# A two-layer hybrid decoder step on one core: the sample group's new convolution columns are copied by ScalarE out of PSUM, query norms get a higher scheduling priority, six weight subtractions move to GpSimd

## The chip, the cores and the metric

The kernel runs on one core of a Trainium2 chip. The metric is the device time of one execution in microseconds (us); the time of a kernel is the median of its runs. Engines are named as the profile names them: PE (TensorE matmul), PEld (its weight loads), DVE (VectorE), ACT (ScalarE), POOL (GpSimd) and SP (SyncE, here a queue that starts DMAs). A q behind a name (ACTq, SPq) is the engine's sequencer, which starts DMAs.

## The reference

Two layers of a decoder trunk run on 544 tokens: a prompt of 512 and a sample group of 8 sequences with 4 new tokens each (32). Each layer is, in short:

```python
mod = silu(c) @ w_ada + b_ada                         # shift, scale and gate, per sequence
h = rmsnorm(x, norm1) * (1 + sc1) + sh1
q, k, v, qi, ki, wi, pool_u, z, xbc, dt_raw, gates = split(h @ w_in)
q = rope(rmsnorm(q, q_norm), pos)                     # the query norms
o_attn = sparse_attention(q, k_all, v_all, qi, ki_all, wi, pos, topk)
o_pool = pool_mix(pool_u, ...)
xbc, conv_state = causal_dwconv(xbc, conv_prev, conv_w, conv_b)    # width 4
o_ssd = ssd_mix(z, silu(xbc), dt_raw, h0, ...)
x = x + g1 * ((sum of gated branches) @ w_out)
h2 = rmsnorm(x, norm2) * (1 + sc2) + sh2
u, fconv_state = causal_dwconv(h2 @ ffn_up, fconv_prev, ffn_conv_w, ffn_conv_b)   # width 3
a, gg = split(u)
x = x + g2 * ((silu(gg) * a) @ ffn_down)
```

A causal convolution of the sample group reads the 3 (or 2) columns of each sequence's saved state and the 4 new columns behind them.

## The kernel before, in words

Activations lie with channels on the 128 partitions and the 544 tokens along the row, in two halves of 272 columns. PE does all products with weights in fp32 by three fp32r products: `weights` (L348 to L358) loads a 128x1024 tile by an SP DMA into a buffer `raw` (4 buffers, also used for tiles of w_ada and for key-value pages), ACT copies the high part `wh` (L177, the line of a helper for copies), DVE subtracts and gives the low part `wl` (L357); `wh` and `wl` have 3 buffers each. `gemm` (L360 to L373) multiplies one weight tile: 8 blocks x 3 products x 2 halves are 48 matmuls of 272 columns into one PSUM tile `psg`, of which there are 2 (L126, L185). `gemm2` (L375 to L392) does two weight tiles side by side at the start of a stage; its matmuls have line L388. It is called by `project` (in layer 0 with tiles prepared earlier) and by `ffn` for its first pair.

`conv` (L886 to L905) takes a finished `psg`. ACT copies it to `cu` (L177) and writes the scaled start of the sum `cacc` (L894). POOL copies the 32 new sample columns of `cu` into the tile `sti` behind the saved state (L896), and the last columns into `sto` (L897), which goes out. DVE adds the shifted products: L901 for the prompt, L904 for the sample columns, from `sti`. It runs 136 times: 24 tiles of xbc and 44 of the feed-forward, per layer. Then ACT takes the tanh `th` (L910) of those that need SiLU, and DVE multiplies (L911). In the feed-forward, tiles come in pairs, `a` and `gg`; every fourth pair a new `sti` is taken, and 8 small DMAs on ACT's queue load the saved state into it (L1628).

`ada` (L238 to L283) computes the modulation of a later stage from w_ada in pieces between other work: a generator loads tiles of w_ada (L255), multiplies them with the conditioning (L262, on PE), and is moved on one step by `pump` at the start of each `gemm`. A norm at a stage's end ends in an inverse square root by three Newton rounds on DVE (L304 to L312; L309 to L311 are one round); its result goes to PE (L468). In `attention`, the query norms use the same rounds; the sample group's factors are then copied by DVE to `qbc` (L1369) and transposed by PE (L1374). At that time DVE also runs the top-k search for the sample group: MAX8 (L861) and MATCH_REPLACE8 (L862) in turn.

The order of instructions on each engine is set by a scheduler when the kernel is built: it goes by modelled times, and by priorities where more than one instruction is ready. `high_priority(offset=WPRI)` lifts what stands under it. Each engine then works in its order; an instruction that waits holds what is behind it.

Of the kernel before, what the change touches and what calls it, by code (L numbers as in the profile page):

```python
# [103 lines left out]
class Prog:  # L104
# [134 lines left out]
    def ada(self, l, s, first=False):  # L239
# [8 lines left out]
        for c in range(4):  # L248
            ps = self.P("ada1")
            for pair in range(2):  # L250
                raws = []
                for z in (2 * pair, 2 * pair + 1):
                    with self.tc.high_priority(offset=WPRI):
                        raw = self.wr.tile([128, 1024], F32, name="raw", tag="raw")
                        nc.sync.dma_start(raw, a["w_ada"][l, s, 4 * c + z])  # L255
                    raws.append(raw)
                    if z % 2 == 0:
                        yield

                prods = []  # L260
                for k4 in range(4):
                    prods.append(nc.tensor.matmul(ps[32 * k4:32 * k4 + 32, :], self.sc[:, 4 * pair + k4, :],  # L262
                                     raws[k4 // 2][:, (k4 % 2) * 512:(k4 % 2) * 512 + 512],
                                     start=(pair == 0), stop=(pair == 1)))
                if pair == 0:
                    if turn:
                        turn(prods[-1].ins)
                        turn = None
                    yield
            if turn:  # L270
                turn(prods[-1].ins)
            row = self.t("adarow")
            self.copy("ada2", row[:, :512], ps)
            turn = self.ada_turn(row, dst[:, c], bias[:, c], first)
            if first or c == 3:
                turn(None)
                turn = None
            yield
# [68 lines left out]

    def weights(self, src, n):  # L348
        nc = self.nc
        z = self.nw = (self.nw + 1) % 4  # L350
        with self.tc.high_priority(offset=WPRI):
# [4 lines left out]
            self.copy("weights2", wh[:, :n], raw[:, :n])  # L356
            self.last_wl = self.E("weights1").tensor_tensor(wl[:, :n], raw[:, :n], wh[:, :n].bitcast(F32), op=OP.subtract).ins  # L357
        return wh, wl  # L358
# [15 lines left out]

    def gemm2(self, srcs, rhs, done=None):  # L375

# [3 lines left out]
        K = len(rhs)  # L380
        ws, self.pre = self.pre or [self.weights(src, K * 128) for src in srcs], None
        os_ = [self.G() for _ in srcs]
# [206 lines left out]
    def project(self):  # L589
        nc, a, l = self.nc, self.a, self.l  # L590
        par, mod, _ = self.par[l]
        h = self.h
        o, ok = self.gemm2([self.w(l, W_KI), self.w(l, W_K)], h)
        kd, self.ki = self.t("kd"), self.t("ki")
# [293 lines left out]
    def conv(self, o, par, wb, nt, bb, st, so, i, width):  # L888
# [5 lines left out]
        nc.scalar.activation(self.v2(acc), self.g2(o), AF.Identity, scale=wb[:, W - 1:W], bias=bb)  # L894
        new = u[:, 512:].rearrange("p (b t) -> p b t", b=8)
        self.E("conv1").tensor_copy(st[:, i, :, W - 1:], new)  # L896
        self.E("conv2").tensor_copy(so[:, i, :], u[:, 513 - W:])  # L897
# [403 lines left out]
    def attention(self):  # L1301
# [29 lines left out]
        def qnorm(sqs, c0):  # L1331
            mk = yield from self.ssq(sqs, "mq")
            self.newton(mk, self.s([128, 5, 8], "rsq_u8"), rq[:, :, c0:c0 + 8])
            yield
# [33 lines left out]
        for p in range(2):  # L1368
            self.E("attention7").tensor_copy(bc[p][:32, :512].rearrange("p (i e d) -> p i e d", i=4, e=2),  # L1369
                                  rq[:32, 4, 8 * p:8 * p + 8].rearrange("p (i e) -> p i e", e=2)[:, :, :, None]  # L1370
# [239 lines left out]
    def ffn(self):  # L1610
# [7 lines left out]
        for ci, n in enumerate(CH):  # L1618
            fs = []
            for jj in range(n):  # L1620
# [8 lines left out]
                if j == 0:  # L1629
                    o, o2 = self.gemm2([self.w(l, W_UP), self.w(l, W_UP + 1)], h)  # L1630
                else:
                    o = self.gemm(self.w(l, W_UP + 2 * j), h)
# [200 lines left out]
```

## Time and profile before

| what | value |
|---|---|
| median of 3 runs | 3163.01 us (3154.23 to 3165.09) |
| profiled execution, its own time | 3159.91 us |
| its span | 3158.1 us |
| PE busy | 3037.2 us (96%), 24136 matmuls |
| DVE, ACT, POOL busy | 71%, 40%, 28% |
| mean granted TensorE clock | 0.98 |

The span is the profile's own, from the first instruction to the last; 1.8 us lie around it. The profiled execution is 3.1 us below the median of the runs. Busy shares are means over all stages.

### The profile page before, as it was taken

The page shows a single profiled execution, that of the slowest core. Times are in us where ns is not written, and L with a number is a line of the kernel's source. Part 1 is how long each engine was busy: PE and PEld are TensorE (multiplying, and loading weights), DVE is VectorE, ACT ScalarE, POOL GpSimd, SP SyncE. Part 2 cuts the span into 40 slices and gives each one's busy share as a digit, 9 for nine tenths or more (in the row PEclk, how much of TensorE's full clock was granted, in tenths as well). Part 3 has the DMA queues.
Part 4 walks back from the last instruction along what each step waited for, and adds up shares of the span by engine and source line. Part 5 has one row for each costly group of instructions (what it writes and reads, how often), then busy time and mean ns, then how long its engine had stood idle before and what let it go on. Part 6 is the DMA issues. An engine that isn't in the chain of part 4 may idle for free. (4 is left out here: it accounts for less than half of the span.)

```text
span 3158.1 us, 62620 instructions
## 1 busy us (share of the span) xinstructions
PE 3037.2 (96%) x24136; PEld 2791.9 (88%) x24136; DVE 2235.4 (71%) x4879; ACT 1261.9 (40%) x2240; POOL 881.0 (28%) x1273
## 2 busy tenths in 40 slices
PE   7999999999999999999989999999999899999999
PEld 4987998999986789998989878989999857899999
DVE  5687878679988656454566878786799885564554
ACT  4344443333336534343443344343333364342432
POOL 1363445521121003111223635455211110121211
PEclk9999999999999999999999999999999899999999
DMA  6332332345543443545333323223333244333322
GB/s 234 107 110 75 113 95 99 113 137 185 190 125 122 162 143 102 162 153 170 94 117 107 107 78 116 93 90 123 99 132 116 79 136 152 98 90 90 86 97 76
DMA packets 303100, 376.81 MB, mean 119 GB/s; under 512 B 177362, under 2 KB 186930, under 8 KB 302802
## 3 DMA queue, kind: packets, MB, share of 16 engines
q1 hardware_dynamic: 116514, 315.94, 29.7%
q10 hardware_dynamic: 181216, 42.05, 6.6%
q0 software_dynamic: 5072, 14.83, 1.3%
q8 instruction: 190, 3.11, 0.4%
q14 instruction: 108, 0.88, 0.1%
HBM read 330.34 MB, written 33.79 MB: 115 GB/s over the span
## 5 line engine op out<-in xcount | busy, mean ns | idle before, releaser
L371 PE MATMUL psg<-hh,wh 128*128 128x272 f32 x4064 | 859.0, 291 | 9.1 <-ACT cacc L894 4.9
L177 ACT ACTIVATE wh<-raw 128x1024 fp32r<-128x1024 f32 (+2 forms) x434 | 425.0, 980 | 1107.1 <-PE psg L371 752.1
L371 PE MATMUL psg<-hl,wh 128*128 128x272 f32 x4064 | 850.0, 289 | 0.0
L371 PE MATMUL psg<-hh,wl 128*128 128x272 f32 x4064 | 847.6, 290 | 0.0
L357 DVE TENSOR_TENSOR wl<-raw,wh 128x1024 fp32r<-128x1024 f32 (+2 forms) x434 | 509.5, 1174 | 334.2 <-ACT wh L177 329.6
L371 PEld LDWEIGHTS psg<-hh,wh 128*128 128x128 f32 x4064 | 642.8, 190 | 35.4 <-issue 14.0
L371 PEld LDWEIGHTS psg<-hh,wl 128*128 128x128 f32 x4064 | 640.4, 189 | 9.8 <-issue 7.2
L371 PEld LDWEIGHTS psg<-hl,wh 128*128 128x128 f32 x4064 | 640.4, 190 | 6.8 <-issue 4.7
L896 POOL COPY sti<-cu 128x32 f32<-128x32 f32 x136 | 85.4, 628 | 522.7 <-ACT cu L177 522.5
L901 DVE SCALAR_TENSOR_TENSOR cacc<-cu,half,cacc 128x511 f32<-128x511 f32 x144 | 137.4, 954 | 5.9 <-ACT cacc L894 4.9
L910 ACT ACTIVATE th<-cacc 128x544 f32<-128x544 f32 x92 | 60.4, 656 | 199.7 <-DVE cacc L904 179.8
L371 PE MATMUL psg<-fh,wh 128*128 128x272 f32 x648 | 133.9, 290 | 2.6 <-DVE resid L495 2.6
L371 PE MATMUL psg<-fl,wh 128*128 128x272 f32 x648 | 133.7, 288 | 0.0
L371 PE MATMUL psg<-fh,wl 128*128 128x272 f32 x648 | 133.6, 288 | 0.0
L489 DVE SCALAR_TENSOR_TENSOR x<-psg,mod,x 128x272 f32<-128x272 f32 x64 | 32.0, 499 | 140.5 <-PE psg L371 131.4
L371 PE MATMUL psg<-oh,wl 128*128 128x272 f32 x512 | 110.1, 291 | 0.0
L371 PE MATMUL psg<-ol,wh 128*128 128x272 f32 x512 | 109.4, 291 | 0.0
L371 PE MATMUL psg<-oh,wh 128*128 128x272 f32 x512 | 109.3, 292 | 0.0
L371 PEld LDWEIGHTS psg<-fh,wh 128*128 128x128 f32 x648 | 100.8, 188 | 8.6 <-PE psg L371 3.4
L1638 POOL TENSOR_TENSOR cacc<-cacc 128x544 f32<-128x544 f32 x44 | 62.2, 1414 | 154.5 <-DVE cacc L911 154.5
L1041 POOL TENSOR_TENSOR seg<-seg,cb 128x512 f32<-128x512 f32 x64 | 89.9, 1407 | 52.5 <-ACT seg L1040 39.3
L911 DVE SCALAR_TENSOR_TENSOR cacc<-th,cacc 128x544 f32<-128x544 f32 x92 | 72.8, 792 | 42.7 <-ACT th L910 42.5
(481 smaller groups left out, 6180.0 us busy)
## 6 DMA issues: line engine op xcount, KB each, us to landing
raw<-wk SPq DMA_DIRECT2D x326, 512.0 KB, 3.3
raw<-w_ada SPq DMA_DIRECT2D x96, 512.0 KB, 4.3
h<-h SPq DMA_DIRECT2D x64, 256.0 KB, 4.5
raw<-wk SPq DMA_DIRECT2D x64, 256.0 KB, 2.8
o_ssds<-hn ACTq DMA_DIRECT2D x64, 256.0 KB, 2.1
raw<-wd SPq DMA_DIRECT2D x32, 448.0 KB, 3.4
kvr<-ckv SPq DMA_DIRECT2D x48, 256.0 KB, 4.0
kvw<-ckv SPq DMA_DIRECT2D x48, 256.0 KB, 3.9
```

Of the source, the lines that this page charges most:

```text
L177: self.nc.scalar.activation(out, src, AF.Copy)
L357: self.last_wl = self.E("weights1").tensor_tensor(wl[:, :n], raw[:, :n], wh[:, :n].bitcast(F32), op=OP.subtract).ins
L371: nc.tensor.matmul(o[:, c, :HC], w[:, k * 128:(k + 1) * 128], x[:, c * HC:(c + 1) * HC], start=(k == 0 and first), stop=(k == K - 1 and last))
L489: self.E("resid1").scalar_tensor_tensor(x[:, :HC], o[:, 0, :HC], g[:, 0:1], x[:, :HC], op0=OP.mult, op1=OP.add)
L896: self.E("conv1").tensor_copy(st[:, i, :, W - 1:], new)
L901: self.E("conv3").scalar_tensor_tensor(acc[:, s:512], u[:, :512 - s], wc, acc[:, s:512], op0=OP.mult, op1=OP.add)
L910: nc.scalar.activation(th, acc, AF.Tanh)
L911: self.E("silu21").scalar_tensor_tensor(acc, th, 1.0, acc, op0=OP.add, op1=OP.mult)
L1041: self.E("ssd_chain5").tensor_tensor(d[:, :512], d[:, :512], cb[:, :512], op=OP.mult)
L1638: self.E("ffn3").tensor_tensor(s_, s_, aa, op=OP.mult)
```

## The change

It has five edits. (1) `ada` issues the DMAs of both tiles of a pair before it yields, and yields once more before their matmuls; before, it yielded between the two loads. (2) `weights` can subtract on POOL; `gemm2` passes this on for `project` and for the first pair of `ffn`: three calls with two tiles each. (3) `conv` writes the new sample columns into `sti` by an ACT copy from PSUM, in place of POOL's copy from `cu`. (4) The Newton rounds of the query norms stand under a priority of 2 x WPRI. (5) So do the two copies to `qbc`.

```diff
@@ ada
                     raws.append(raw)
-                    if z % 2 == 0:
-                        yield
+                yield
@@ weights
-    def weights(self, src, n):
+    def weights(self, src, n, eng=None):
...
-            self.last_wl = self.E("weights1").tensor_tensor(wl[:, :n], raw[:, :n], wh[:, :n].bitcast(F32), op=OP.subtract).ins
+            eng = eng or self.nc.vector
+            if eng is self.nc.gpsimd:
+                eng.tensor_tensor(wl[:, :n], raw[:, :n], wh[:, :n].bitcast(F32), op=OP.subtract)
+                return wh, wl
+            self.last_wl = eng.tensor_tensor(wl[:, :n], raw[:, :n], wh[:, :n].bitcast(F32), op=OP.subtract).ins
@@ gemm2: weights(src, K * 128, eng); project and the first pair of ffn pass eng=nc.gpsimd
@@ conv
-        new = u[:, 512:].rearrange("p (b t) -> p b t", b=8)
-        self.E("conv1").tensor_copy(st[:, i, :, W - 1:], new)
+        self.copy("conv6", st[:, i, :, W - 1:], o[:, 1, 512 - HC:HC].rearrange("p (b t) -> p b t", b=8))
@@ attention, qnorm
-            self.newton(mk, self.s([128, 5, 8], "rsq_u8"), rq[:, :, c0:c0 + 8])
+            with self.tc.high_priority(offset=2 * WPRI):
+                self.newton(mk, self.s([128, 5, 8], "rsq_u8"), rq[:, :, c0:c0 + 8])
@@ attention
-            self.E("attention7").tensor_copy(bc[p][:32, :512].rearrange("p (i e d) -> p i e d", i=4, e=2),
+            with self.tc.high_priority(offset=2 * WPRI):
+                self.E("attention7").tensor_copy(bc[p][:32, :512].rearrange("p (i e d) -> p i e d", i=4, e=2),
```

The scheduler orders all engines anew. Lines of the changed kernel are 2 to 4 higher than before from L344 on. Three places show what moves.

The first is ACT in the feed-forward of layer 0, at the start of its second group of pairs: `cu`, `cacc` of tile `a`, the loads of the new `sti`, then tile `gg`. Before:

```order
L177 ACTIVATE cu<-psg 128x544
L894 ACTIVATE cacc<-psg,par 128x544
L177 ACTIVATE fh<-cacc 128x544
L1628 DMA sti<-st_ffn 128x8x2 x3
L177 ACTIVATE wh<-raw 128x1024
L1628 DMA sti<-st_ffn 128x8x2 x5
L177 ACTIVATE cu<-psg 128x544
L894 ACTIVATE cacc<-psg,fhalf 128x544
```

With the change:

```order
L177 ACTIVATE cu<-psg 128x544
L897 ACTIVATE cacc<-psg,par 128x544
L177 ACTIVATE fh<-cacc 128x544
L1632 DMA sti<-st_ffn 128x8x2 x3
L177 ACTIVATE wh<-raw 128x1024
L1632 DMA sti<-st_ffn 128x8x2 x2
L177 ACTIVATE wh<-raw 128x1024
L1632 DMA sti<-st_ffn 128x8x2 x3
L177 ACTIVATE sti<-psg 128x8x4
L177 ACTIVATE cu<-psg 128x544
L897 ACTIVATE cacc<-psg,fhalf 128x544
L177 ACTIVATE sti<-psg 128x8x4
```

The new copy of tile `a` (the first `sti<-psg`) stands behind all loads of the new `sti` and two `wh`; that of tile `gg` directly behind its `cacc`.

The second is SP's loads in the same stretch, with the semaphores that they wait for. Before:

```order
L255 DMA raw_15946<-w_ada 128x1024 [waits DMAHW3_49,DMAHW0_49,DVE_49]
L353 DMA raw_15960<-wk8 128x1024 [waits DMAHW4_49,DMAHW2_49,DVE_49]
L255 DMA raw_16033<-w_ada 128x1024 [waits DMAHW7_49,DMAHW5_49,PE_49]
L353 DMA raw_16035<-wk8 128x1024 [waits DMAHW6_49,DMAHW4_49,DVE_49]
L255 DMA raw_16100<-w_ada 128x1024 [waits DMAHW6_49,DVE_49]
L353 DMA raw_16108<-wk8 128x1024 [waits DMAHW1_49,PE_49]
```

With the change:

```order
L352 DMA raw_15883<-wk8 128x1024 [waits DMAHW7_49,DMAHW3_49,DVE_49]
L352 DMA raw_15960<-wk8 128x1024 [waits DMAHW4_49,DMAHW0_49,DVE_49]
L255 DMA raw_16033<-w_ada 128x1024 [waits DMAHW5_49,DMAHW3_49,DVE_49]
L255 DMA raw_16035<-w_ada 128x1024 [waits DMAHW6_49,DMAHW4_49,DVE_49]
L352 DMA raw_16037<-wk8 128x1024 [waits DMAHW1_49,PE_49]
L352 DMA raw_16108<-wk8 128x1024 [waits DMAHW2_49,PE_49]
```

Tiles of w_ada and weight tiles came in turn; now they come in pairs, and a pair of weight tiles waits for PE, whose L261 (L262 before) reads the w_ada tiles that hold the buffers.

The third is DVE in the attention of layer 1, from the squares' mean `mq` of the second query norm to the first copy to `qbc`. Before:

```order
L544 TENSOR_SCALAR mq<-psa 32x8
L357 TENSOR_TENSOR wl<-raw,wh 128x1024
L862 MATCH_REPLACE wks<-mxs,wks 32x1028
L306 TENSOR_SCALAR rsq_u_30674<-mq 128x40
L861 MAX mxs<-wks 32x8
L307 TENSOR_SCALAR rq<-rsq_u_30674 128x5x8
L862 MATCH_REPLACE wks<-mxs,wks 32x1028
L309 TENSOR_TENSOR rsq_u_30674<-rq 128x40
L1369 COPY qbc_30810<-rq 32x512
```

With the change:

```order
L547 TENSOR_SCALAR mq<-psa 32x8
L360 TENSOR_TENSOR wl<-raw,wh 128x1024
L864 MAX mxs<-wks 32x8
L305 TENSOR_SCALAR rsq_u_30674<-mq 128x40
L865 MATCH_REPLACE wks<-mxs,wks 32x1028
L306 TENSOR_SCALAR rq<-rsq_u_30674 128x5x8
L864 MAX mxs<-wks 32x8
L308 TENSOR_TENSOR rsq_u_30674<-rq 128x40
L1373 COPY qbc_30810<-rq 32x512
```

Between `mq` and `qbc` there are three search steps as before, in another turn; over the whole order one MATCH_REPLACE fewer stands ahead of this copy (29, not 30).

## Rows read from the trace of the kernel before

**Rows 1.** The page's busy times of each engine.

```profile
PE 3037.2 (96%) x24136; PEld 2791.9 (88%) x24136; DVE 2235.4 (71%) x4879; ACT 1261.9 (40%) x2240; POOL 881.0 (28%) x1273
```

**Rows 2.** Waits of PE, whole span: total us, times, longest.

```profile
PE psb L1161 <- DVE hn L1167: 14.7, 5, 3.8
...
PE psb L1374 <- DVE qbc L1369: 9.5, 2, 8.6
...
PE psa L468 <- DVE rstdh L311: 8.5, 4, 3.8
...
PE psg L371 <- ACT cacc L894: 4.9, 4, 1.6
```

**Rows 3.** Groups by line and form: busy, mean ns | idle before, releaser.

```profile
L896 POOL COPY sti<-cu 128x32 f32<-128x32 f32 x136 | 85.4, 628 | 522.7 <-ACT cu L177 522.5
...
L177 ACT ACTIVATE exs<-psg 128x32 f32<-128x32 f32 x16 | 3.2, 203 | 0.0
```

**Rows 4.** Timeline, state-space mixer of layer 0: start, us, engine, line.

```profile
491.89 2.57 DVE L904 SCALAR_TENSOR_TENSOR cacc<-sti,half,cacc 128x32 f32<-128x32 f32 x3 [3.20 <-POOL sti L896]
...
491.64 0.21 POOL L896 COPY sti<-cu 128x32 f32<-128x32 f32 x1
...
495.11 0.50 PE L1161 MATMUL psb<-sxst,bbd 96*128 96x512 f32 x1 [3.39 <-DVE hn L1167]
...
496.47 0.52 PE L371 MATMUL psg<-hh,wh 128*128 128x272 f32 x2 [0.86 <-ACT cacc L894]
```

**Rows 5.** Windows: busy us of PE, PEld, DVE, ACT, POOL, granted clock, DMA.

```profile
496.00:500.00 4.00, 3.53 (x17) 3.53 (x18) 4.00 (x7) 3.63 (x6) 3.08 (x8) 0.62 0.51 194
500.00:504.00 4.00, 4.00 (x31) 3.92 (x31) 3.81 (x6) 0.92 (x2) 3.84 (x3) 0.96 0.38 133
...
508.00:512.00 4.00, 4.00 (x34) 4.00 (x33) 3.50 (x14) 1.17 (x2) 0.42 (x2) 1.00 0.20 66
...
1200.00:1204.00 4.00, 3.28 (x26) 3.28 (x27) 4.00 (x7) 2.83 (x4) 2.38 (x4) 1.00 0.36 131
```

**Rows 6.** Timeline of DVE, a search step of layer 1.

```profile
2484.19 1.20 DVE L862 MATCH_REPLACE8 wks<-mxs,wks 32x1028 f32<-32x1028 f32 x1
```

**Rows 7.** Timeline of DVE and POOL at the end of layer 0.

```profile
1616.81 1.23 DVE L357 TENSOR_TENSOR wl<-raw,wh 128x1024 fp32r<-128x1024 f32 x1 [0.22 <-ACT wh L177]
...
1629.83 0.65 DVE L309 TENSOR_TENSOR rsq_u<-rstdh 128x3 f32<-128x3 f32 x1
...
1629.69 0.77 POOL L452 TENSOR_TENSOR hl<-hn,hh 128x272 fp32r<-128x272 f32 x1 [3.89 <-ACT hh L177]
```

**Rows 8.** Timeline of DVE and PE ahead of the feed-forward of layer 0.

```profile
1170.02 0.15 DVE L311 SCALAR_TENSOR_TENSOR rstdh<-rsq_u,rstdh 128x3 f32<-128x3 f32 x1
...
1172.87 1.92 PE L262 MATMUL psb<-raw,sc 128*32 128x512 f32 x4 [4.47 <-DMA raw<-w_ada]
1174.72 1.69 PE L468 MATMUL psa<-cst,rstdh 128*128 128x128 f32 x6
```

**Rows 9.** Timeline of ACT and PE, feed-forward of layer 0, first place.

```profile
1248.95 6.49 ACTq L1628 DMA_DIRECT2D sti<-st_ffn  x5
1255.48 0.63 ACT L177 ACTIVATE cu<-psg 128x544 f32<-128x544 f32 x1 [5.48 <-issue]
...
1257.77 0.64 PE L262 MATMUL psb<-raw,sc 128*32 128x512 f32 x4
```

**Rows 10.** Timeline of ACT and PE, second place.

```profile
1415.66 0.63 ACT L177 ACTIVATE cu<-psg 128x544 f32<-128x544 f32 x1 [1.17 <-issue]
...
1419.15 1.07 PE L262 MATMUL psb<-raw,sc 128*32 128x512 f32 x8
```

**Rows 11.** Timeline of ACT, first place of layer 1.

```profile
2816.02 1.06 ACT L177 ACTIVATE wh<-raw 128x1024 fp32r<-128x1024 f32 x1 [3.33 <-PE psg L371]
...
2818.19 0.63 ACT L177 ACTIVATE cu<-psg 128x544 f32<-128x544 f32 x1 [1.11 <-issue]
```

**Rows 12.** DMA issues from 1190 to 1480 us: count, KB, median us to landing.

```profile
raw<-wk SPq DMA_DIRECT2D x32, 512.0 KB, 4.0
```

More of the change, by code (lines that the diff above doesn't have):

```diff
@@ L373, in gemm, with gemm2 @@
         return o
-    def gemm2(self, srcs, rhs, done=None):
+    def gemm2(self, srcs, rhs, done=None, eng=None):
         nc = self.nc
@@ L380, in gemm2 @@
         K = len(rhs)
-        ws, self.pre = self.pre or [self.weights(src, K * 128) for src in srcs], None
+        ws, self.pre = self.pre or [self.weights(src, K * 128, eng) for src in srcs], None
         os_ = [self.G() for _ in srcs]
@@ L592, in project @@
         h = self.h
-        o, ok = self.gemm2([self.w(l, W_KI), self.w(l, W_K)], h)
+        o, ok = self.gemm2([self.w(l, W_KI), self.w(l, W_K)], h, eng=nc.gpsimd)
         kd, self.ki = self.t("kd"), self.t("ki")
@@ L1629, in ffn @@
                 if j == 0:
-                    o, o2 = self.gemm2([self.w(l, W_UP), self.w(l, W_UP + 1)], h)
+                    o, o2 = self.gemm2([self.w(l, W_UP), self.w(l, W_UP + 1)], h, eng=nc.gpsimd)
                 else:
```

## The prediction

> **What bounds the kernel now.** I read the page first: PE is busy 96% of the span, DVE 71%, ACT 40%, POOL 28% [rows 1]. So the end is set by PE, and only what shortens PE's stalls, or the half-speed stretches after them, is worth time. Then the list of PE's waits, which names who ends them: the state-space mixer's `hn` on DVE (14.7 us), the first copy to `qbc` (one wait of 8.6), the inverse square root at stage ends (8.5), ACT's `cacc` (4.9) [rows 2]. The windows tell what a stall costs behind itself: after the 3.39 us stall that ends at 495.11, the window from 496 has a granted clock of 0.62 (a mix of the levels 1.2 and 2.4 GHz, which are 0.5 and 1.0) and 17 matmuls in 3.53 busy us, the next 0.96 and 31, where an undisturbed one has 34 [rows 4, 5]. At 34 in 4 us a matmul is 0.118 us apart (0.124 inside one weight tile); the 13 and 3 missing are 2.0 us. The longest wait for `cacc`, 1.6 us [rows 2], ends at 1200.7, and there the clock stays at 1.00 [rows 5]. So a stall of three us or more costs about two more, one of 1.6 nothing more.
>
> **What the change gives.**
> *New columns by ACT, third group of the mixer.* DVE idles 3.20 us for POOL's copy, which starts at 491.64 although it takes 0.21: it stood behind other POOL work [rows 4]. Behind it `hn` is late, PE stalls 3.39 us, and 0.86 more on `cacc` at 496.47 [rows 4]. With ACT's copy directly behind `cacc`, that wait goes. POOL still writes its own part of `hn`, so I leave 0.7 of the 3.4. Gain 2.7 + 0.86 + 2.0 of clock = 5.6, and the same group in layer 1 has the like: **11.1 us**. Late next is POOL's `hn`.
> *Second group.* Its stall is the 3.8 us among five [rows 2]; there POOL's copy is only one of several POOL pieces, 0.63 us each on average [rows 3]. 2 x 0.63 = **1.3 us**; bounds 0 and 2 x (3.8 + 2.0).
> *Query norms.* The priority doesn't bring the rounds together: three search steps still stand between `mq` and `qbc`, since a round's step waits for the one before and a ready search step slips in. One MATCH_REPLACE8 of 1.20 us fewer stands ahead of the copy [rows 6]: **1.2 us** of 8.6; bounds 0 and all of it with its clock, 10.6.
> *Subtractions to POOL.* At three stage ends one subtraction of 1.23 us less lies ahead of the Newton rounds [rows 7]. About half is on the path, 3 x 0.6 = **1.8 us**. Against it: at 1629.83 a round's step of usually 0.15 [rows 8] took 0.65 and ended with POOL's `hl`, which ran from 1629.69 for 0.77 [rows 7]. A POOL subtraction is not in this trace; by columns from that `hl`, 0.77 x 1024 / 272 = 2.9 us at most, 1.23 at least. I take **1 us** of loss in all, as two of three rounds can start behind it; bounds 0 and 3 x 2.9 = 8.7. The Trainium skill, "SBUF — State Buffer", section "Who interferes with whom", says that a VectorE instruction with two SBUF inputs is shut out for the whole length of a GpSimd instruction that reads SBUF and started first. By it every subtraction that starts in front of a round would cost its full length, the upper bound; the row at 1629.83, which ends where POOL ends, agrees.
> *w_ada pairs, good side.* At 1172.87 PE comes out of a 4.47 us wait for a tile of w_ada; the norm's matmul L468 stands behind it, at 1174.72, though its factor was ready at 1170.17 [rows 8]. In the new order only matmuls of an earlier loaded pair stand ahead of L468. 1174.72 - 1170.17 = **4.5 us**; bounds 0 and 6.5 with clock. For the start of the program, where the first tiles are also fetched earlier, **1 us**.
> Gains: 11.1 + 1.3 + 1.2 + 1.8 + 4.5 + 1 = 20.9.
>
> **What it costs.**
> *ACT's copies themselves.* The nearest row, a 128x32 copy from PSUM by ACT, takes 203 ns [rows 3]; 136 are 27.6 us on an engine 40% busy. It shows where PE waits for ACT to free a `psg` (4 waits before [rows 2]): 4 x 0.2, about **1 us**.
> *The copy that stands behind loads.* A `psg` is now free only when this copy has read it. At six places, the second group of pairs in each third of the feed-forward, both layers, the copy of tile `a` stands behind six or eight loads of the new state and one or two `wh`. There are two `psg`: `gg` fills the other, and the product after it needs the one of `a`. Before, `cacc` was its last reader, and the loads delayed only `cu` of `gg`, which had a whole product's time. First place: the eight loads let `cu` of `gg` start at 1255.48, after 5.48 us of waiting for issue; the product that follows `gg` ended with L262 at 1257.77 and so began 48 x 0.124 = 5.95 earlier, 1251.8 [rows 9]. The new order puts four L262 rows (1.07 us [rows 10]) in front of it: 1252.9. The copy ends at 1255.48 + 0.2 at the earliest: PE waits 2.8. Second place: 1419.15 - 5.95 + 1.07 = 1414.3 against 1415.66 + 0.2: 1.6 [rows 10]. First of layer 1: `wh`, which waits for PE to end `gg`, starts at 2816.02, and `cu` at 2818.19 [rows 11]: 2.4. At the other three one `wh` and one load stand between: 1.06 + 0.2, 1.3 each. Sum 2.8 + 1.6 + 2.4 + 3.9 = 10.7, and 1.5 of clock behind the longest: **12.2 us**. Bounds: a `wh` and a copy everywhere, 6 x 1.3 = 8; eight loads at 6.49 / 5 = 1.3 us each [rows 9] against a product's 5.95, 6 x (4.5 + 2) = 39.
> *w_ada pairs, bad side.* A pair of weight tiles now waits for the L262 that frees two `raw`, and the first of it is wanted one product later, where it was two before; eleven times in the feed-forward of layer 0. From the L262 to the low part: 4.0 us landing [rows 12], 1.06 `wh` [rows 11], 1.23 `wl` [rows 7], 6.3; the product between takes 5.95. 11 x 0.4 = **4.4 us**; bounds 0 and, with 1.5 us of queueing on ACT and DVE more, 11 x 1.9 = 21.
> Costs, with the 1 us of POOL: 1 + 1 + 12.2 + 4.4 = 18.6.
>
> **The sum.** 3159.9 of the profiled execution - 20.9 + 18.6 = 3157.6. That execution lies 3.1 us under the median of the runs shown, so the median would be 3160.7, **3161 us**. About 0.3% (9.5 us, below 3153.5 or above 3172.5) is what a measurement of this kernel can tell from no change: the forecast is no change.
>
> **The rivals.**
> *The loads are cheap.* ACT's loads wait for semaphores that the new order deals out anew; if they issue without waiting, the six stalls shrink to the lower bound, 8 us without clock, and the pairs cost nothing. 12.2 - 8 + 4.4 = 8.6, with the second group's stalls half gone, 2 x 2.9 - 1.3 = 4.5: 3161 - 13 = 3148. For it: in layer 1 only one load and a `wh` hold the copy at most places. Against: 1.3 us a load at the first place.
> *The query norm comes in time.* The change then does there what it says: 10.6 - 1.2 = 9.4, and the second wait of 0.9 with it: 3161 - 10 = 3151. Against: the order above.
> *The held `psg` decides, slower.* Place: the six group starts. If all are as long as the first one's loads allow, with clock, the price is between 12.2 and 39; at the middle, 26, the time is 3161 + 14 = 3175. It decides as soon as the copy ends over 3 us behind `gg`'s product. For it: 5.48 us of issue at the first place.
> *The pairs run dry, slower.* At the upper bound, 21 - 4.4 = 17: 3178. The point is a landing over 4 us: 4.0 is the median, so half of them.
> *POOL shuts DVE out.* By the rule cited above, 8.7 - 1 = 8 more, 3169: still no change alone.
>
> **How the numbers follow.** The forecast, with POOL's rival in it, 0.42. Faster: cheap loads 0.18, query norm 0.13, together 0.31. Slower: held `psg` 0.14, pairs 0.13, together 0.27. The forecast's own range is 3154 to 3172. The range for 8 in 10 takes in the middles of all rivals and somewhat of their tails, where gains or costs fall together: 3140 to 3182.
>
> **What would show it.** Right: no wait of L1161 near 495 and 2080 over 1 us; a wait of about 7.4 us for `qbc`; L468 without w_ada ahead; six new waits of PE for ACT's copy to `sti`, 1.3 to 3 us each, at the second group of each third of the feed-forward; DVE's `cacc` never waiting for POOL. Wrong: these six absent, or over 4 us with half clock; PE waiting for `wh` or `wl` in the feed-forward of layer 0; newly slow Newton rounds beside POOL's `wl`.

## The result: slower by 0.76%, and the profile of the changed kernel

The changed kernel takes 3181.68 us (median of 6 runs, 3178.33 to 3190.49), the kernel before on the same chip 3160.14 us. The ratio is 1.0076, with a 95% interval of 1.0059 to 1.0093. The forecast was no change, at 3161; the range up to 3182 just holds the time. In the profile the span grew by 21.0 us, to 3179.1.

First the page of the changed kernel, busy times of each engine (busy us, share, instructions):

```profile
PE 3044.9 (96%) x24136; PEld 2799.4 (88%) x24136; DVE 2228.7 (70%) x4873; ACT 1272.7 (40%) x2376; POOL 862.7 (27%) x1143
```

Beside [rows 1]: PE is 7.7 us busier with the same number of matmuls, which I read as stretches at the lower clock behind new stalls (one is shown below); the rest of the 21.0 is idle time. ACT, with 136 instructions more, is 10.8 us busier, POOL 18.3 us less. Now who PE waits for (us in total, times, longest; the first line is left out, a wait of 14.1 us for the first norm's squares at the program's start, the same in both kernels):

```profile
...
PE psg L374 <- ACT sti L177: 14.3, 8, 3.4
PE psb L1163 <- DVE hn L1169: 13.9, 4, 4.2
PE psb L1378 <- DVE qbc L1373: 12.3, 2, 6.8
PE psa L471 <- DVE rstdh L310: 10.4, 4, 5.0
PE psa L1022 <- DVE cb L1010: 9.9, 2, 4.9
```

Lines from `weights` on have moved by 2 to 4: L374 is the product of [rows 2]'s L371, L1163 was L1161, L1378 was L1374, L471 was L468. Three things stand beside [rows 2]. ACT's copy to `sti` is a new wait of 14.3 us, where `cacc` had 4.9. The wait for `hn`, which I had expected to lose two of its five, is 13.9 instead of 14.7. And `qbc` has a new wait: this 6.8 is in layer 0, where PE did not wait for it at all; of layer 1's two, 8.6 and 0.9, one of 5.5 is left.

The new wait at its longest, in the timeline of ACT and PE, feed-forward of layer 0, the first place of the prediction:

```profile
1256.96 4.40 ACTq L1632 DMA_DIRECT2D sti<-st_ffn  x3
...
1261.41 0.20 ACT L177 ACTIVATE sti<-psg 128x32 f32<-128x32 f32 x1 [3.40 <-DMA sti<-st_ffn]
...
1261.66 0.52 PE L374 MATMUL psg<-hh,wh 128*128 128x272 f32 x2 [3.40 <-ACT sti L177]
```

The copy itself takes 0.20 us. It starts when the loads in front of it in ACT's order have been issued, and PE starts 0.25 behind it.

The third group of the mixer in layer 0, in the timelines of DVE, POOL and PE (the place of [rows 4]):

```profile
482.81 0.99 DVE L903 SCALAR_TENSOR_TENSOR cacc<-cu,half,cacc 128x511 f32<-128x511 f32 x1 [0.46 <-ACT cacc L897]
483.72 1.03 DVE L906 SCALAR_TENSOR_TENSOR cacc<-sti,half,cacc 128x32 f32<-128x32 f32 x1
484.67 0.74 DVE L903 SCALAR_TENSOR_TENSOR cacc<-cu,half,cacc 128x510 f32<-128x510 f32 x1
485.33 1.02 DVE L906 SCALAR_TENSOR_TENSOR cacc<-sti,half,cacc 128x32 f32<-128x32 f32 x1
486.28 0.74 DVE L903 SCALAR_TENSOR_TENSOR cacc<-cu,half,cacc 128x509 f32<-128x509 f32 x1
486.94 1.02 DVE L906 SCALAR_TENSOR_TENSOR cacc<-sti,half,cacc 128x32 f32<-128x32 f32 x1
487.89 0.67 DVE L1169 TENSOR_TENSOR hn<-hn,psb 128x512 f32<-128x512 f32 x1
...
483.21 3.09 POOL L1143 TENSOR_TENSOR bbd<-bh,cst 32x512 fp32r<-32x512 f32 x2
486.37 1.55 POOL L1143 TENSOR_TENSOR bbd<-bl,cst 32x512 fp32r<-32x512 f32 x1
...
488.62 0.79 PE L1163 MATMUL psb<-sxst,bbd 96*128 96x512 f32 x1 [3.09 <-DVE hn L1169]
```

The wait of DVE for POOL's copy is gone, as the diff says. But DVE now does its six pieces beside POOL's `bbd`, and a piece of 32 columns takes 1.02 us. The six last 5.08 us, the group's first `hn` stands behind them, and PE waits 3.09 us for it. Before, the six were spread out. In DVE's timeline the first `hn` stood ahead of all six and the second between them, and PE's stall of 3.39 came further on, behind the last three [rows 4]:

```profile
481.17 0.67 DVE L1167 TENSOR_TENSOR hn<-hn,psb 128x512 f32<-128x512 f32 x1
481.76 3.83 DVE L901 SCALAR_TENSOR_TENSOR cacc<-cu,half,cacc 128x511 f32<-128x511 f32 x3
485.51 0.67 DVE L1167 TENSOR_TENSOR hn<-hn,psb 128x512 f32<-128x512 f32 x1
```

So the scheduler dealt out DVE's order anew here, and the stall moved. It is as long in layer 1: 4.21 us where it was 3.41. The pieces themselves did not become dearer. Before, three and three took 3.83 and 2.57 us, 6.4 in all, beside POOL as well. Over the whole kernel the mixer's pieces of 32 columns (before, then with the change) lose their idle time ahead of them, and their mean stays:

```profile
L904 DVE SCALAR_TENSOR_TENSOR cacc<-sti,half,cacc 128x32 f32<-128x32 f32 x144 | 76.2, 529 | 6.6 <-POOL sti L896 6.4
...
L906 DVE SCALAR_TENSOR_TENSOR cacc<-sti,half,cacc 128x32 f32<-128x32 f32 x144 | 76.5, 531 | 0.0
```

### The profile page after: what moved, and what is told of

Same layout as the page of the kernel before. It is cut to its first block, busy times and chain, and to the rows that moved or that the text cites. A ratio compares the mean times of both kernels' runs of the same rounds, so it can differ in the third digit from the quotient of the medians.

```text
span 3179.1 us, 62638 instructions
## 1 busy us (share of the span) xinstructions
PE 3044.9 (96%) x24136; PEld 2799.4 (88%) x24136; DVE 2228.7 (70%) x4873; ACT 1272.7 (40%) x2376; POOL 862.7 (27%) x1143
## 3 DMA queue, kind: packets, MB, share of 16 engines
q8 instruction: 190, 3.11, 0.4%
## 4 chain that ended last, share of the span: by engine, by line
PE 73%; DVE 8%; issue 3%; DMA 3%; ACT 2%; POOL 1%; ACTq 1%; SPq 0%; DVEq 0%; POOLq 0%
PE psg L374 58%; PE psg L391 2%; PE psb L261 1%; DVE wl L360 1%; PE psb L1063 1%; DMA raw<-wk 1%; PE psb L1465 1%; DVE cacc L903 1%; ACT wh L177 1%; DVE cacc L906 1%; PE psb L1049 1%; PE psa L1460 1%; DMA kvr<-ckv 1%; PE psg L1525 1%; PE psg L1437 1%
## 5 line engine op out<-in xcount | busy, mean ns | idle before, releaser
L374 PE MATMUL psg<-hh,wh 128*128 128x272 f32 x4064 | 857.0, 291 | 18.5 <-ACT sti L177 14.3
L374 PE MATMUL psg<-hl,wh 128*128 128x272 f32 x4064 | 857.2, 291 | 0.0
L374 PE MATMUL psg<-hh,wl 128*128 128x272 f32 x4064 | 851.7, 290 | 0.0
L374 PEld LDWEIGHTS psg<-hh,wh 128*128 128x128 f32 x4064 | 644.4, 190 | 43.6 <-ACT sti L177 18.5
L374 PEld LDWEIGHTS psg<-hh,wl 128*128 128x128 f32 x4064 | 643.8, 190 | 10.3 <-issue 6.4
L374 PEld LDWEIGHTS psg<-hl,wh 128*128 128x128 f32 x4064 | 642.4, 190 | 9.0 <-issue 7.4
L899 POOL COPY sto<-cu 128x34 f32<-128x34 f32 (+1 forms) x136 | 79.7, 586 | 555.8 <-ACT cu L177 555.4
L374 PE MATMUL psg<-fh,wh 128*128 128x272 f32 x648 | 134.0, 289 | 2.6 <-DVE resid L498 2.6
L374 PE MATMUL psg<-fl,wh 128*128 128x272 f32 x648 | 133.9, 288 | 0.0
L374 PE MATMUL psg<-fh,wl 128*128 128x272 f32 x648 | 133.9, 288 | 0.0
L374 PE MATMUL psg<-ol,wh 128*128 128x272 f32 x512 | 110.5, 292 | 0.0
L374 PE MATMUL psg<-oh,wl 128*128 128x272 f32 x512 | 109.9, 291 | 0.0
L374 PE MATMUL psg<-oh,wh 128*128 128x272 f32 x512 | 109.7, 293 | 0.0
L374 PEld LDWEIGHTS psg<-fh,wh 128*128 128x128 f32 x648 | 101.0, 188 | 7.6 <-PE psg L374 3.4
L374 PEld LDWEIGHTS psg<-fh,wl 128*128 128x128 f32 x648 | 101.2, 188 | 1.7 <-DVE wl L360 0.8
L177 ACT ACTIVATE cu<-psg 128x544 f32<-128x544 f32 x136 | 83.2, 612 | 46.5 <-PE psg L374 39.4
```

The costliest lines, as they stand in the source:

```text
L177: self.nc.scalar.activation(out, src, AF.Copy)
L374: nc.tensor.matmul(o[:, c, :HC], w[:, k * 128:(k + 1) * 128], x[:, c * HC:(c + 1) * HC], start=(k == 0 and first), stop=(k == K - 1 and last))
```

## The experiments

The ratio is always to the kernel before on the same chip, with its 95% interval. In us I give (ratio - 1) x 3160. An interval that reaches 1 is not clear of no change.

### Each edit alone

Edit 1, the pairs:

```diff
                     raws.append(raw)
-                    if z % 2 == 0:
-                        yield
+                yield
```

> The kernel before with one edit alone: both tiles of w_ada of a pair are fetched together. Theory A (the pairs starve VectorE in the query stage of layer 0): PE's wait for the first `qbc` of layer 0, 6.8 us in the changed kernel and none before, appears here too, with some 3 us of half clock behind it, against 7 gained at the stage end near 1175: about +3 us in all, 3163. Rival B (that wait belongs to another edit): no such wait, only the gain of 7 at the stage end: 3153.

Measured: 3162.3 us, 1.0013 (1.0000 to 1.0025), +4 at the edge of its interval. Theory A is nearest. The wait for `qbc` in layer 0 is there, at 4.43, but the gain at the stage end is not: PE still waits 4.35 us for a tile of w_ada there.

```profile
920.16 3.61 PE L1373 MATMUL psb<-cst,qbc 32*128 32x32 f32 x16 [4.43 <-DVE qbc L1368]
...
1180.29 1.92 PE L261 MATMUL psb<-raw,sc 128*32 128x512 f32 x4 [4.35 <-DMA raw<-w_ada]
```

Edit 2, the subtractions (with `eng` passed on by `weights` and `gemm2`):

```diff
-        o, ok = self.gemm2([self.w(l, W_KI), self.w(l, W_K)], h)
+        o, ok = self.gemm2([self.w(l, W_KI), self.w(l, W_K)], h, eng=nc.gpsimd)
...
-                    o, o2 = self.gemm2([self.w(l, W_UP), self.w(l, W_UP + 1)], h)
+                    o, o2 = self.gemm2([self.w(l, W_UP), self.w(l, W_UP + 1)], h, eng=nc.gpsimd)
```

> The kernel before with one edit alone: POOL makes the low parts of the two tiles of weights at three stage ends. Theory A: a Newton round that begins beside POOL's subtraction is stretched; the wait at 1635 grows by 1.2 us and two waits for `kbc` of 1.0 and 2.2 us, which the changed kernel has and the one before has not, appear here: +3 to +5 us. Rival B: these belong to the edit of the new columns or to the query norms, and VectorE's 1.23 us per subtraction are gained at the three ends: -2 us.

Measured: 3155.0 us, 0.9987 (0.9973 to 1.0000), -4, on B's side and also at the edge. The stage end that I had given to the pairs is cured here. In PE's timeline the norm's matmul now stands ahead of w_ada, and the tile of w_ada is hardly waited for, beside 4.47 in [rows 8]:

```profile
1163.80 0.26 PE L472 MATMUL psa<-cst,rstdh 16*128 16x16 f32 x1
...
1165.62 1.92 PE L262 MATMUL psb<-raw,sc 128*32 128x512 f32 x4 [0.22 <-DMA raw<-w_ada]
```

A wait of 2.2 us for `kbc` near 1690 appears in this kernel, in those of edits 1 and 3 and of the priorities: no one edit owns it.

Edit 3, ACT's copy:

```diff
-        new = u[:, 512:].rearrange("p (b t) -> p b t", b=8)
-        self.E("conv1").tensor_copy(st[:, i, :, W - 1:], new)
+        self.copy("conv6", st[:, i, :, W - 1:], o[:, 1, 512 - HC:HC].rearrange("p (b t) -> p b t", b=8))
```

> The kernel before with one edit alone: ACT writes the new columns from PSUM. Theory A (this edit is most of the loss): eight PE waits for ACT's copy to `sti`, 14.3 us in all in the changed kernel, and the third groups of the mixer lose 3 and 6 us instead of gaining 5.6 each: +18 us, 3178. Rival B: the waits for the copy appear, 11 us in the feed-forward, but the third groups gain as forecast (-11): 0. Rival C: the third groups neither gain nor lose: +11, 3171.

Measured: 3179.6 us, 1.0063 (1.0046 to 1.0081), +20. Theory A: this edit carries most of the loss. Ten waits for the copy, 15.6 us.

Edits 4 and 5, the priorities:

```diff
+            with self.tc.high_priority(offset=2 * WPRI):
...
+            with self.tc.high_priority(offset=2 * WPRI):
```

> The kernel before with the two priorities alone: the Newton rounds of the query norms and the copies to `qbc`. Theory A: layer 1 gains 5 us (its wait for `qbc` 5.5 instead of 8.6), layer 0 has no wait for it, as before: 3155. Rival B (the priorities themselves make the new wait of layer 0, by putting the rounds in front of low parts of weights that PE needs sooner): a wait for `qbc` near 920 with some 3 us of half clock, +8, against 5 gained in layer 1: 3163.

Measured: 3159.9 us, 0.9999 (0.9983 to 1.0015): nothing. The wait in layer 1 is 5.7 instead of 8.6, and there is none in layer 0, as Theory A has it; of the 5 us nothing can be seen in the time. Nor can the shorter wait be put down to the priorities: it is 6.0 with edit 2 alone and 5.5 with edit 3 alone, which don't have them, and 8.55, as before, in a kernel further on that has them (the whole change with ACT's copy ahead).

The four alone sum to +6.2 per mille, against +7.6 (5.9 to 9.3) for all: they add, within the intervals.

### Edit 3 taken apart

The feed-forward alone has ACT's copy where the width is 3, the mixer alone where it is 4:

```diff
-        new = u[:, 512:].rearrange("p (b t) -> p b t", b=8)
-        self.E("conv1").tensor_copy(st[:, i, :, W - 1:], new)
+        if W == 3:
+            self.copy("conv6", st[:, i, :, W - 1:], o[:, 1, 512 - HC:HC].rearrange("p (b t) -> p b t", b=8))
+        else:
+            new = u[:, 512:].rearrange("p (b t) -> p b t", b=8)
+            self.E("conv1").tensor_copy(st[:, i, :, W - 1:], new)
```

> The kernel before with ACT's copy of the new columns in the feed-forward alone (104 of 136 would be there by rows of the page; the mixer keeps POOL's copy). Theory A (the copy that stands behind the state loads holds `psg`): eight waits of PE for ACT's copy, 12 us by their sum with the edit alone, and the waits for `cacc` of the feed-forward (1.6 the longest) gone: +9 us. Rival B (the loss of this edit, 20 us, comes from the mixer): within 3 us of before.

(The number 104 in it is an error of mine: 88 of the 136 places are in the feed-forward.) Measured: 3174.0 us, 1.0042 (1.0030 to 1.0054), +13. Nine waits for the copy in the feed-forward sum to 13.0 us, while those for `cacc` fall from 4.9 to 1.7.

> The kernel before with ACT's copy in the mixer alone; the feed-forward keeps POOL's. Theory A (ACT's copy behind a low-priority place and the third groups' VectorE work now beside POOL's): two waits for the copy of 1.8 us, third groups 3 us later each, +8 to +10 us. Rival B (the mixer gains what was forecast, 11 us in the third groups, once the feed-forward is left alone): -8 us.

Measured: 3164.5 us, 1.0012 (0.9999 to 1.0025), +4, not clear of no change. No gain of 11 in the mixer, and half the loss of Theory A. The two waits of 1.8 are there, and the third groups' stalls for `hn` are 3.11 and 4.61 us.

Then the copy's place alone, first for edit 3, then in the whole changed kernel:

```diff
+        with self.tc.high_priority(offset=WPRI):
-        self.copy("conv6", st[:, i, :, W - 1:], o[:, 1, 512 - HC:HC].rearrange("p (b t) -> p b t", b=8))
+            self.copy("conv6", st[:, i, :, W - 1:], o[:, 1, 512 - HC:HC].rearrange("p (b t) -> p b t", b=8))
```

> The kernel before with ACT's copy everywhere, but with a priority that puts it right behind `cacc` at all 136 places, ahead of the state loads, of `seg` and of the copies of weights. Theory A (the place of the copy in ACT's order is the cost): the waits for the copy, 15.6 us in ten places, fall below 0.5 us each, so some 12 of the 20 us come back: 3166. Rival B (what costs is that VectorE and POOL now run beside each other, or the order of PE that the scheduler deals out anew): 3176 or more.

> The changed kernel with one thing mended: ACT's copy of the new columns gets a priority that puts it right behind `cacc` at all 136 places. Theory A (the place of the copy, behind state loads and copies of weights, is most of the loss, here as with the edit alone, where it was 15 of 20 us): 3166, and the waits of PE for the copy at the feed-forward's group starts gone. Rival B (in the whole change the loss is that of the pairs and the third groups): 3176 or more.

Measured: 3165.8 us, 1.0013 (0.9997 to 1.0029), with edit 3 alone, 16 us less than 1.0063; and 3164.8 us, 1.0015 (1.0004 to 1.0025), in the whole change, 19 less than 1.0076. The times are Theory A's both times. Its waits are not all: with edit 3 alone four waits for the copy stay (2.40, 2.39, 1.69 and 1.57 us), at the third groups and at the start of each feed-forward, where before `cacc` had 0.86 and 1.6. ACT's timeline at the first place, the whole change with this one thing mended:

```profile
1247.63 0.80 ACT L897 ACTIVATE cacc<-psg,par 128x544 f32<-128x544 f32 x1
...
1248.87 0.20 ACT L177 ACTIVATE sti<-psg 128x32 f32<-128x32 f32 x1
...
1254.01 3.70 ACTq L1633 DMA_DIRECT2D sti<-st_ffn  x3
1257.76 0.63 ACT L177 ACTIVATE cu<-psg 128x544 f32<-128x544 f32 x1 [2.70 <-DMA sti<-st_ffn]
```

The copy starts 0.44 us behind the end of `cacc`, where it came 10 us behind it. The last three loads still hold ACT's order for 3.70 us (4.40 in the changed kernel), but now in front of the next tile's `cu`, as before the change. What stays is the mixer's: with edit 3 alone PE waits 2.40 for the copy in the third group and 0.72 and 1.69 for `hn`, 4.8 together, against 3.39 + 0.86 in [rows 4]. In this kernel the first `hn` again stands ahead of the six pieces (486.23 against 486.82), and the waits for `hn` are 2.4 instead of 3.4.

```profile
479.35 0.65 PE L371 MATMUL psg<-hh,wh 128*128 128x272 f32 x2 [2.40 <-ACT sti L177]
...
493.42 0.49 PE L1161 MATMUL psb<-sxst,bbd 96*128 96x512 f32 x1 [0.72 <-DVE hn L1167]
499.59 0.50 PE L1161 MATMUL psb<-sxst,bbd 96*128 96x512 f32 x1 [1.69 <-DVE hn L1167]
```

### The mixer with POOL's `bbd` taken away

ACT makes `bbd` in four pieces each, so POOL has 48 products less; the products themselves are the same.

```diff
-                self.E("ssd_sample7").tensor_tensor(
-                    bbd.bitcast(F32R)[32 * r:32 * r + 32, :512].rearrange("p (b n) -> p b n", b=4),
-                    src[:, None, :].to_broadcast([32, 4, 128]), bm, op=OP.mult)
+                for z in range(4):
+                    nc.scalar.activation(bbd.bitcast(F32R)[32 * r:32 * r + 32, 128 * z:128 * z + 128], src, AF.Identity,
+                                         scale=c[:32, C_BM + 4 * hf + z:C_BM + 4 * hf + z + 1])
```

> The kernel with ACT's copy right behind `cacc` (4.9 us slower than before), and POOL's products `bbd` made by ACT in four pieces each instead. Theory A (VectorE and POOL take turns; the wait for POOL's copy was replaced by turns of 0.8 us in front of six small pieces): `cacc` pieces of 32 columns in the third group take 0.24 us but beside `hn`, the stall for `hn` after it and that for the copy shrink to under 1.5 us each, and the kernel comes out 5 us or more below its like without this: 3160. Rival B (the third group is bound by the order of PE or by ACT): the stalls stay within 0.5 us of what they were.

> The control: the kernel before with `bbd` made by ACT. Theory A: POOL's copy comes earlier with less ahead of it, so this one gains too, 3 us at each third group: 3155; and the difference to e3e_bbd falls from 4.9 us to under 2. Rival B: no change, or a loss from 192 more pieces of ACT.

Measured: with ACT's copy right behind `cacc` 3148.7 us, 0.9966 (0.9951 to 0.9981), where it had 1.0013; the control 3152.9 us, 0.9977 (0.9966 to 0.9988). So the kernel with ACT's copy gains 15 us by it (6 to 16 below the kernel before, where it was 1 below to 9 above), the control 7 (4 to 11), and a disadvantage of 4 becomes an advantage of 3.5 (that last difference is within the intervals). In neither does PE wait over 0.8 us in the third group. The waits of the second groups go as well, from 3.8 us (3.3 with ACT's copy) to 0.8 and less, so not all of the gain is the third groups'. DVE and POOL there, with ACT's copy:

```profile
482.06 1.03 DVE L904 SCALAR_TENSOR_TENSOR cacc<-sti,half,cacc 128x32 f32<-128x32 f32 x1
...
484.78 0.74 DVE L901 SCALAR_TENSOR_TENSOR cacc<-cu,half,cacc 128x510 f32<-128x510 f32 x1
485.44 0.24 DVE L904 SCALAR_TENSOR_TENSOR cacc<-sti,half,cacc 128x32 f32<-128x32 f32 x1
485.60 0.74 DVE L901 SCALAR_TENSOR_TENSOR cacc<-cu,half,cacc 128x509 f32<-128x509 f32 x1
486.26 0.25 DVE L904 SCALAR_TENSOR_TENSOR cacc<-sti,half,cacc 128x32 f32<-128x32 f32 x1
...
470.64 12.39 POOL L1164 TENSOR_TENSOR hn<-h,dac 128x512 f32<-128x512 f32 x8
482.98 0.21 POOL L897 COPY sto<-cu 128x35 f32<-128x35 f32 x1
```

The same instruction takes 1.03 while POOL's `hn` runs and 0.24 once POOL is through. A pair of L901 and L904 then takes 0.82 (484.78 to 485.60), three 2.5, where the changed kernel needed 5.08. The run takes two things away together, DVE's turns with `bbd` and POOL's own time, and the scheduler orders DVE anew a third time; how the gain divides stays open. With `bbd` off POOL the stalls go with either copy; that ACT's copy brought the turns the two runs do not show.

### The pairs

> The changed kernel without the first edit: the tiles of w_ada are fetched one by one again. Theory A (the edits add up; the pairs cost 4 us by themselves, with a new wait for `qbc` in layer 0): 3177, and no wait for `qbc` near 920 over 1 us, while the stage end near 1175 keeps its gain, since that one is POOL's subtraction's. Rival B (the pairs gain 7 us at the stage end in company of the others): 3185 or more.

Measured: 3178.9 us, 1.0050 (1.0032 to 1.0068). The wait for `qbc` in layer 0 falls to 1.34 us and the stage end keeps its gain, as Theory A has it, in a time that is 8 us below the whole change's by the ratios, with intervals that overlap.

In the kernel of edit 1 alone ACT waits up to 9.3 us for a raw tile between 600 and 925 us (before: 6.3). I put this down to the pair, which takes two of the four buffers at once, though in sum these waits hardly change (53.0 us in 14, before 52.5 in 13). So the next two runs give five:

```diff
-            self.wr = pool("wraw", 4)
+            self.wr = pool("wraw", 5)
...
-BUFS = {"T": 54, "U": 10, "R": 1, "V": 2}
+BUFS = {"T": 52, "U": 10, "R": 1, "V": 2}
```

> The first edit alone, with five buffers for raw weights instead of four (and 52 slots for activations instead of 54, to make room). Theory A (a pair takes two of four buffers at once, so the tiles of the products come in bursts, ACT waits up to 9.3 us for one, VectorE gets its low parts late and the query norm with it): with a fifth buffer the waits of ACT for a raw tile between 600 and 925 us shrink below 7 us each and PE's wait for `qbc` near 920 falls from 4.4 us to under 1; against the kernel before with the same buffers within 3 us. Rival B (the order that the scheduler gave VectorE, not the loads): the wait for `qbc` stays at 4 us or more.

> The control for that: the kernel before with five raw buffers and 52 activation slots. Theory A: loads were hardly late before, so -2 to +2 us. Rival B (two slots fewer bind): +5 us or more.

Measured: 3156.0 us, 0.9982 (0.9969 to 0.9994), with the pairs; 3141.8 us, 0.9942 (0.9928 to 0.9955), without. My theory fell, twice. (The control's longest such wait is 8.3 us, above the 6.3 of four buffers, and it is the fastest of the four: the longest wait says little.) With the pairs ACT's waits for raw tiles in that stretch shrink from 53.0 us in 14 to 31.5 in 6, but the wait for `qbc` stays, and the pairs now cost 13 us, three times as much. And the control is no control but the largest gain of a single edit: -18 us. Part of it lies where the change was aimed. With POOL's copy and POOL's `bbd` in place, PE's waits for `hn` and `cacc` in the two third groups (3.39 + 0.86 in [rows 4] and the like in layer 1) are gone; 1.80 and 1.60 us for DVE's `secs` are left. POOL's copy stands right behind `bbd` there, ahead of POOL's products for `hn` (484.38 against 484.70). No run separates this from the fifth buffer's other effects. PE in layer 0, with five buffers and no pairs:

```profile
486.18 0.47 PE L1161 MATMUL psb<-sxst,bbd 96*128 96x512 f32 x1 [1.80 <-DVE secs L1171]
```

What of the pairs costs is open: it isn't the waits for raw tiles alone. PE's wait for `qbc` in layer 0 is 0 before, 3.15 with five buffers, 4.45 with the pairs and five:

```profile
914.13 3.59 PE L1373 MATMUL psb<-cst,qbc 32*128 32x32 f32 x16 [4.45 <-DVE qbc L1368]
```

I read this as a place without slack: the wait shows also in the kernel with ACT's copy in the feed-forward alone (2.99), which touches nothing near it but the order.

### Versions that beat both kernels

Edits 2, 4 and 5 without the others:

> The change without its first and third edit: POOL's subtractions and the query norms' priorities alone. Theory A (the edits add up): -4 us for POOL, 0 for the priorities, 3154. Rival B (the priorities put rounds ahead where POOL's subtraction then stands in their way): 3160 or more.

Measured: 3156.0 us, 0.9984 (0.9970 to 0.9999): the gains of the parts, as Theory A has it.

> POOL's subtractions and the query norms' priorities, without pairs and without ACT's copy, with five raw buffers. Theory A (independent gains add): -20 for the buffer and -5 for the edits: 3136. Rival B (both cure the same waits, the stage end near 1175 above all): 3141, as the buffer alone.

Measured: 3143.2 us, 0.9948 (0.9929 to 0.9967). Rival B: with the fifth buffer these edits add nothing (0.9942 without them).

> The kernel before with six raw buffers and 50 activation slots. Theory A (the fifth buffer took most waits for raw tiles away): within 4 us of five buffers, 3142. Rival B (raw tiles still bind): 3130 or less. Rival C (50 slots bind): 3150 or more.

Measured, with `pool("wraw", 6)` and 50 slots: 3143.5 us, 0.9951 (0.9934 to 0.9968). Theory A: five are enough.

The last two put together what gained; the first has ACT's copy right behind `cacc`, `bbd` by ACT and five buffers, the second edits 2, 4 and 5 as well:

> The parts that gained, together: ACT's copy right behind `cacc`, `bbd` by ACT, five raw buffers. If the gains add: -12 and -20, 3129. If the buffer and the mixer's edits cure the same waits: 3138 or more.

> The same with POOL's subtractions and the query norms' priorities on top. If these add their 4 to 5 us: 3125. Since with the buffer they added nothing (3143 beside 3142): 3129, as without them.

Measured: 3136.2 us, 0.9928 (0.9911 to 0.9945), and 3139.9 us, 0.9928 (0.9910 to 0.9946). The first lies between its two guesses: of 11 + 18 = 29 us, 23 are there. The second lies above both of its own (3125 and 3129); by the ratios the two kernels are equal. The priorities and POOL's subtractions are worth nothing on top. The page of the first:

```profile
PE 3031.5 (97%) x24136; PEld 2784.3 (89%) x24136; DVE 2209.4 (71%) x4879; ACT 1329.7 (42%) x2568; POOL 798.9 (26%) x1089
```

And two of its waits of PE:

```profile
PE psb L1374 <- DVE qbc L1369: 10.5, 3, 8.5
PE psa L468 <- DVE rstdh L311: 9.5, 5, 3.8
```

PE is 5.7 us less busy than in [rows 1], POOL 82 us; what is left of the waits named here stands at the query norm of layer 1 and at the stage ends. The longest waits for `hn` of [rows 2] are no longer among the first.

## Why the prediction was wrong, step by step

| step of the sum | predicted, us | measured |
|---|---|---|
| third groups | +11.1 gained | waits there from 8.5 to 10.8; the mixer's part alone +4 slower (0 to 8) |
| second groups | +1.3 gained | waits there from 7.6 to 6.6 |
| copy behind state loads, ACT's copies | -13.2 | feed-forward alone +13 slower (9 to 17) |
| pairs, both sides and start | +1.1 | alone +4 slower (0 to 8) |
| POOL's subtractions | +0.8 | alone 4 faster (0 to 9) |
| query norms | +1.2 | alone nothing (5 faster to 5 slower) |

*The step that failed is the first gain*: "With ACT's copy directly behind `cacc`, that wait goes ... Gain 2.7 + 0.86 + 2.0 of clock = 5.6, and the same group in layer 1 has the like". DVE's wait of 3.20 us did go, and PE's stall for `hn` did not: 3.09 us in layer 0 and 4.21 in layer 1, where it was 3.39 and 3.41. The step takes DVE's order as it was and lets `hn` move up by the wait; the prediction has no word on a new order here. In the new order all six pieces stand ahead of the group's first `hn`, 5.08 us, of which three turns with `bbd` make 3 x 0.8 = 2.4; before, that `hn` stood ahead of all six. The turns alone are not what is new, since the pieces had them before (529 ns in the mean, 531 now). With the first `hn` ahead again, as with edit 3 and its copy's priority, the stalls for `hn` are 2.4 us instead of 3.4; with `bbd` off POOL they go. How much of the lost gain is the order's and how much the turns' no run separates.

The 0.86 us for `cacc` did go at its tile. But at another tile, earlier in the group, PE now waits 1.78 us for the copy, and 1.76 in layer 1, where it did not wait before. Here the copy does stand right behind `cacc`, but `cacc` stands behind a copy of weights, in the timelines of ACT and PE of the changed kernel:

```profile
472.13 1.05 ACT L177 ACTIVATE wh<-raw 128x1024 fp32r<-128x1024 f32 x1
473.07 0.80 ACT L897 ACTIVATE cacc<-psg,half 128x544 f32<-128x544 f32 x1
473.76 0.20 ACT L177 ACTIVATE sti<-psg 128x32 f32<-128x32 f32 x1
...
474.02 0.61 PE L374 MATMUL psg<-hh,wh 128*128 128x272 f32 x2 [1.78 <-ACT sti L177]
```

So with the copy's priority raised these two waits don't shrink (2.40 there).

*The copy behind the loads* was right in place and cause, and near in size. Five of six places show it (3.40, 1.37, 2.73, 1.10 and 0.98 us; I had 2.8, 2.4 and 1.3 each), the second of layer 0 not. They sum to 9.6 us, for 10.7 forecast. With the copy ahead of the loads these waits are gone. My rival "the held `psg` decides" took this to be longer than forecast; it was not. What decided is that the gains which were to stand against it did not come. That the stated range still holds the time is luck: its upper end came from rivals that did not happen.

*The pairs.* The good side was wrongly attributed: the stage end is cured by POOL's subtraction, with the pairs alone the wait is 4.35 of 4.47. The bad side was looked for in the feed-forward of layer 0; PE waits for no weights there. It came in front of the query norm of layer 0, where I had no wait to go by. The forecast had priced a stall of three us or more at two us of clock behind it; behind this one of 6.80 the clock is at 0.50 for ten us (below), which by my estimate costs half of that, 5 us.

*POOL's subtractions* take 2.39 us each, between my bounds of 1.23 and 2.9. And they do shut DVE out, in the timeline of the changed kernel:

```profile
1628.73 2.44 DVE L305 TENSOR_SCALAR rsq_u<-msh 128x3 int32<-128x3 int32 x1
...
1628.77 2.38 POOL L358 TENSOR_TENSOR wl<-raw,wh 128x1024 fp32r<-128x1024 f32 x1
...
1634.83 1.76 PE L471 MATMUL psa<-cst,rstdh 128*128 128x128 f32 x6 [5.05 <-DVE rstdh L310]
```

A step that takes 0.17 elsewhere ends with POOL's subtraction, and PE's wait grew from 3.80 to 5.05 (5.03 to 5.06 in every kernel with edit 2, 3.80 or 3.81 in every one without). Each of the six subtractions holds one DVE instruction in this way, which takes 2.37 to 2.45 us. So it went as the Trainium skill has it ("SBUF — State Buffer", "Who interferes with whom"): on the ports that the two engines share, the instruction that comes second waits until the first is through. (By that section an instruction with one SBUF input is held only in the two-port modes; this one has one, and no run here shows its mode.) The 1.02 us of the third group, on instructions with two inputs, agree with it as well. I had cited it for the subtractions alone and had not asked where else DVE stands beside POOL. That would have led to the third group. In price the subtractions seem to gain all the same (0 to 9 us alone), by the stage end near 1175.

*Query norms.* In layer 1 the wait fell by 3.1 us, more than the 1.2 forecast, but no run shows this to be the priorities' doing. Over all the kernels built here it takes either 5.4 to 6.0 us or 8.5 (once 7.1), and both with and without the priorities. In layer 0 it is new, with the clock at 0.50 behind it:

```profile
925.12 3.62 PE L1378 MATMUL psb<-cst,qbc 32*128 32x32 f32 x16 [6.80 <-DVE qbc L1373]
```

```profile
925.00:930.00 5.00, 4.88 (x22) 0.50 0.34 107
930.00:935.00 5.00, 5.00 (x24) 0.50 0.02 5
```

(The second fence has two windows: busy us of PE and matmuls, granted clock, DMA share, GB/s.) Of its 6.80 us, 1.34 are left without the pairs.

## What to carry to other kernels

A wait that one engine has for another is a gain only if what the bottleneck waits for moves up with it: before booking it, write down what stands ahead of that instruction in the new order, and take the price of each from a place where it already runs beside the other engine. A cheap instruction that frees a buffer belongs right behind the last reader, whatever its engine; ask what stands ahead of it in the queue, not what it takes. And a control with one buffer more can be worth more than the whole change under study.

## What the runs showed of the hardware that I had not expected

DVE's 32-column piece takes 0.24 us with POOL idle. Of the 320 pieces of the kernel before, 54 take longer, 0.38 to 1.35 us, and every one of them ends 0.04 to 0.05 us behind the end of a POOL instruction. In the changed kernel there are 54 again, of which the same holds. Most (31 before, 37 after) take 1.00 to 1.05 us, about the length of one of POOL's products. POOL's side stretches too: `bbd` on 32x512 takes 1.04 us alone and in many cases 1.55 beside DVE. And POOL's blocked time did not go away with the instruction: the copy to `sti` that was removed stood at 628 ns [rows 3]; the copy to `sto` behind it then took that place, and went from 255 ns to 586:

```profile
L899 POOL COPY sto<-cu 128x34 f32<-128x34 f32 (+1 forms) x136 | 79.7, 586 | 555.8 <-ACT cu L177 555.4
```
